# Gate of the delta branch applied in its PSUM bank, with the first operands of the output product taken from there, and a third up-projection job started early

## The chip, the cores and the metric

The kernel runs on one core of a Trainium2 chip, in one launch. The metric is the device time of one execution in microseconds (us), from the start of the program to its end. A profile of one execution gives the span from the first to the last instruction, the time of every instruction on its engine, and what each engine waited for. The engines are PE (TensorE, matrix products), PEld (its weight loads, which overlap the products), DVE (VectorE), ACT (ScalarE), POOL (GpSimd) and SP (SyncE, which issues nearly all of the DMAs).

## What is computed

One layer of a hybrid encoder on 512 tokens of 1024 channels, in float32:

```
h      = rmsnorm(x);  proj = h @ w_in          # pool | q k v z | gates
y_pool = pooled branch(p) @ pool_out
y_dn   = gated delta rule, both directions, normed @ dn_out
merged = sigmoid(g_pool) * y_pool + sigmoid(g_dn) * y_dn
x      = x + merged @ w_o
h2     = rmsnorm(x)
u      = conv3(h2 @ ffn_up);  x = x + (silu(gate) * value) @ ffn_down
out    = rmsnorm(x)
```

Everything around the change lies between `y_dn` and the first columns of `h2 @ ffn_up`.

## The kernel before

**Three products for one.** Every float32 operand is split into a rounded high part and a low part, the difference. `mm3` (lines 389 to 391) multiplies high by high, high by low and low by high into one PSUM bank. High parts are casts on ACT, low parts are subtractions on POOL or DVE. POOL cannot read PSUM.

**A planner writes the order.** Each step is declared with `A` (ACT), `V` (DVE), `G` (POOL), `M` (PE) or `L` (a DMA issued by SP), with an estimated cost, the names it reads and writes, and a key. The planner plays the program through with these costs; on each engine the ready step with the lowest key goes next. `FEED`, `EVICT` and `CHAIN` are offsets that put a step far ahead of plain keys; FEED goes before EVICT. The engines then run that order, each strictly in sequence, and wait on semaphores that the tile framework sets where instructions touch the same tile. Buffers come from rings: `pp` is a ring of three one-bank PSUM tiles, `raw`, `whi` and `wlo` hold weights (3, 2 and 2), `y` holds five 128x512 tiles, and `ms` two operand sets of the w_o product.

**The stage of `do_unit` (line 1530).** For each of eight channel blocks c, a job of 24 matmuls (8 contraction blocks, `mm3` each) forms a 128x512 block of y_dn in a `pp` bank, `ps_do`. Two loads bring the gate `gd` and the finished product of the pool branch `m1` into `y` tiles; ACT takes the sigmoid of `gd`. Then DVE multiplies the bank by the gate into the `gd` tile in SBUF (line 1546), which frees the bank, and adds `m1` into block c of the merged tile `m` (line 1549).

**The w_o product.** `merged @ w_o` runs as a scheme of seven half-size products, in the order 1, 2, 6, 5, 3, 7, 4 (`W_ORDER`). Each takes sums or differences of quarters of `merged` (tokens 0 to 255 and 256 to 511, channel blocks 0 to 3 and 4 to 7) and of `w_o`. The operands of products 1 and 2 are plain quarters; `s3` (for 7) is a first difference; those of 6, 5 and 3 are made in place in `m` by `mcombine` (line 1620). `msplit` casts an operand on ACT (line 1628) and takes its low part on DVE (line 1632). `wsum` (line 1588) forms the sums of w_o on DVE or POOL, `wsplit` (lines 1601 and 1604) their high and low parts; `LO_BY` says for each product and block which of POOL (G) and DVE (V) takes the low part. Their homes are tiles `ws` a and b and the freed tiles kT and kk.

**Where the products land.** A product has two token blocks j of four groups of `mm3`. Products 1, 6, 3 and 4 use the two banks of a single two-bank tile, `oo`, called `wo` in the trace; 2, 5 and 7 use `pp` banks (`ps_wo`). `wdone` says where each is added: `wplus` adds it to a half row of the residual tile `x2` (line 1753, `x` in the trace); `wkeep` copies product 1 to SBUF tile `wu` on ACT (line 1760); `wmore` adds 6 and 7 to `wu` on DVE (line 1765), and POOL adds `wu` to `x2` three times for each j.

**Into the next norm and the up projection.** `norm2_first` and `norm2_rest` (lines 1694 to 1716) form squares, root, reciprocal and scaled rows for 128 tokens at a time; PE turns them (line 1722), ACT and DVE split them into `h2` (lines 1728 and 1729). The up projection has 44 jobs of 24 matmuls; the first two (`up0_0`, `up0_1`) run in two halves of 256 tokens, since the first 256 tokens are normed before the rest. Each bank is taken by `conv3` (ACT line 1871, DVE line 1877) into a tile of pool `fp`, which `ffn_open` opens when the memory of the earlier stage is free (`tail` lists whose uses it awaits).

Of the kernel before, what the change touches and what calls it, by code (L numbers as in the profile page):

```python
# [14 lines left out]
P = 128  # L15
# [212 lines left out]
def hybrid_block(  # L228
# [55 lines left out]

    def G(cost, fn, r=(), w=(), key=0.0):
        add("pool", cost, fn, r, w, key)

# [135 lines left out]

    def job(src, kt, xs, xr, name, halves=False, pair=False, feed=None, more=0.0):

# [5 lines left out]
        if pair:  # L431
            def load():
                box["raw"] = wpool.tile([P, kt, n], F32, tag="wraw", bufs=RINGS["raw"], name=f"wr_{name}")
                sp.dma_start(box["raw"], src)

            def split():
                w = box["hi"] = wpool.tile([P, kt, 2 * n], F32R, tag="whi", bufs=RINGS["whi"], name=f"wp_{name}")
                act.copy(w[:, :, 0:n], box["raw"])

            def split2():  # L440
                w = box["hi"]
                pool.tensor_tensor(out=w[:, :, n:], in0=box["raw"], in1=f32(w[:, :, 0:n]), op=ALU.subtract)

            whi = f"whi:{name}"
            wlo = whi
            L(128, load, w=[f"raw:{name}"], key=FEED + u)
            A(ca(kt * n), split, r=[f"raw:{name}"], w=[whi], key=FEED + u)
            G(cp(kt * n), split2, r=[f"raw:{name}"], w=[whi], key=FEED + u)
        else:
            wb, whi, wlo = weights(src, kt, n, name, u, feed, more)  # L450
        pp = f"pp:{name}"

        def mmk(k, a, b):
# [3 lines left out]
            if pair:  # L457
# [7 lines left out]
                return  # L465
            mm3(box["ps"][:n, a:b], wb["hi"][:, k, :], wb["lo"][:, k, :], xhi[:, a:b], xlo[:, a:b], k == 0, k == kt - 1)

        spans = [(0, S)] if not halves else [(0, S // 2), (S // 2, S)]
        for i, (a, b) in enumerate(spans):
            for k in range(kt):  # L470
                lo_part = wlo if pair else f"{wlo}#{0 if k < kt // 2 else 1}"
                M((MM3 if not pair else 0.46) / len(spans), lambda k=k, a=a, b=b: mmk(k, a, b),
                  r=[whi, lo_part] + xr(k, a, b), w=[pp], key=u + 50 * i + k, n=4 if pair else 6)
        return box, pp, u
# [1056 lines left out]
    def do_unit(c):  # L1531
# [12 lines left out]

        def mul():
            dve.tensor_tensor(out=b["gd"], in0=box["ps"], in1=b["gd"], op=ALU.mult)

        def plus():
            dve.tensor_tensor(out=mg["m"][:, c, :], in0=b["gd"], in1=b["m1"], op=ALU.add)
# [16 lines left out]
    ADD = EVICT - 60  # L1566
    T_W = (slice(0, 256), slice(256, 512))
    u_wo = {p: next_unit() for p in W_ORDER}
    u_w0 = u_wo[1]
    wsets, wslot = {}, {}  # L1570

# [47 lines left out]
    def mcombine(dst, dstn, x, y, names, op, key, n):  # L1619
        V(cd(256 * n) + 0.22, lambda: dve.tensor_tensor(out=dst(), in0=x(), in1=y(), op=op), r=names, w=dstn, key=key)  # L1620

    def msplit(p, i, n, src, srcn, key):
# [36 lines left out]
    for i in range(0, QK, 2):  # L1659
        msplit(1, i, 2, *mblk(i, 0, 2), FEED + u_w0 + i)  # L1660
        mcombine(*s3(i), mblk(i, 0, 2)[0], mblk(i, 1, 2)[0], mblk(i, 0, 2)[1] + mblk(i, 1, 2)[1], ALU.subtract, FEED + u_w0 + i, 2)
    for i, n in ((0, 2), (2, 1), (3, 1)):
        msplit(2, i, n, *mblk(i + QK, 0, n), FEED + u_wo[2] + i)
    for i in range(0, QK, 2):
        (x, xn), (y, yn), (z, zn) = mblk(i, 0, 2), mblk(i, 1, 2), mblk(i + QK, 1, 2)
        mcombine(y, yn, y, z, yn + zn, ALU.add, FEED + u_wo[6] + i, 2)
        mcombine(x, xn, y, x, xn + yn, ALU.subtract, FEED + u_wo[6] + i, 2)
        msplit(6, i, 2, x, xn, FEED + u_wo[6] + i)
    for i in range(0, QK, 2):
# [77 lines left out]
    def wplus(p, j, th, n, u, eng=V):  # L1747
        t = 2 * th + j
        e, src, sn = (dve, lambda: wacc[p, j], wname(p, j)) if eng is V else (pool, lambda: wacc["u", j], f"y:wu{j}")

        def plus():
            dst = x2[t][:, half(n)]
            e.tensor_tensor(out=dst, in0=src(), in1=dst, op=ALU.add)

        eng(cd(512) if eng is V else cp(512), plus, r=[sn], w=[f"xr{t}#{n}"], key=u)

    def wkeep(j, u):
        def keep():
            wacc["u", j] = y_tile(f"wu{j}")
            act.copy(wacc["u", j], wacc[1, j])  # L1760
# [403 lines left out]
```

## Time and profile before

| what | value |
|---|---|
| median of three timed runs | 887.25 us (887.17 to 890.71) |
| the profiled execution | 886.23 us |
| its span, first to last instruction | 884.5 us |
| PE busy in the span | 867.1 us |
| granted TensorE clock, mean | 0.997 |

The profiled execution lies 1.02 us below the median, and 1.73 us of it lie outside the span. The views used below are the page of the profile, busy times by stretch (windows), the waits of PE, the instructions of a tile with their shortest, median and longest duration, and the timeline: start, duration, engine, line, tiles, and in brackets the idle time before, with what ended it.

### The profile page before, as it was taken

How to read it: one execution, taken by the hardware profiler on the slowest of the kernel's cores; microseconds unless marked ns; L12 is line 12 of the kernel's file. 1: busy time of each engine (PE TensorE's matmuls, PEld its weight loads, DVE VectorE, ACT ScalarE, POOL GpSimd, SP SyncE). 2: the span in 40 equal slices, each digit the busy share in tenths (PEclk: the TensorE clock that was granted, in tenths of full speed). 3: DMA queues.
4: the chain of work that ended last, by engine and by line, in shares of the span. 5: the costliest groups of instructions: out<-in, count | busy, mean ns of one | idle time of the engine just before them, and what ended most of it. 6: DMA issues, size and time to landing. Idle time of an engine off the chain costs nothing.

```text
span 884.5 us, 13820 instructions
## 1 busy us (share of the span) xinstructions
PE 867.1 (98%) x5027; PEld 729.3 (82%) x5027; DVE 602.2 (68%) x1025; ACT 471.1 (53%) x792; POOL 542.2 (61%) x463
## 2 busy tenths in 40 slices
PE   8999999999999999999999889999999999999997
PEld 7888888888888887888877669888888888888886
DVE  5756597367578887554768995565566555569996
ACT  6688544336858533346755555444443333465664
POOL 3445555223646554253699894787778776567763
PEclk9999999999999999999999999999999999999999
DMA  7365446304255463125896004566666675265553
GB/s 208 96 194 144 120 131 155 109 26 131 73 143 154 121 142 86 55 84 168 298 325 220 1 24 144 197 219 202 219 222 214 204 241 180 102 208 185 175 178 147
DMA packets 165511, 138.07 MB, mean 156 GB/s; under 512 B 23662, under 2 KB 133051, under 8 KB 165444
## 3 DMA queue, kind: packets, MB, share of 16 engines
q1 hardware_dynamic: 160706, 135.62, 49.4%
q10 hardware_dynamic: 4738, 1.58, 0.8%
q8 instruction: 39, 0.64, 0.3%
q14 instruction: 28, 0.23, 0.1%
HBM read 113.03 MB, written 24.15 MB: 155 GB/s over the span
## 4 chain that ended last, share of the span: by engine, by line
PE 62%; DVE 3%; ACT 1%; issue 0%; POOL 0%; DVEq 0%
PE ps_up L389 9%; PE ps_up L390 9%; PE ps_up L391 9%; PE dn L389 4%; PE dn L391 4%; PE dn L390 4%; PE ps_do L391 2%; PE ps_do L389 2%; PE ps_do L390 2%; PE ps_gp L389 1%; PE ps_gp L391 1%; PE ps_gp L390 1%; PE ps_p L389 1%; PE ps_po L391 1%; PE ps_po L389 1%; PE ps_po L390 1%
## 5 line engine op out<-in xcount | busy, mean ns | idle before, releaser
L415 POOL TENSOR_TENSOR wl_up<-wr_up,wh_up 128x512 fp32r<-128x512 f32 x88 | 117.0, 1350 | 46.4 <-ACT wh_up L411 46.3
L389 PE MATMUL ps_up<-h_hi,wh_up 128*128 128x512 f32 (+1 forms) x368 | 139.9, 380 | 0.0
L390 PE MATMUL ps_up<-h_lo,wh_up 128*128 128x512 f32 (+1 forms) x368 | 139.8, 380 | 0.0
L391 PE MATMUL ps_up<-h_hi,wl_up 128*128 128x512 f32 (+1 forms) x368 | 139.7, 380 | 0.0
L1877 DVE SCALAR_TENSOR_TENSOR c<-ps_up,fw,c 128x511 f32<-128x511 f32 x88 | 66.0, 750 | 98.1 <-ACT c L1871 92.0
L2066 POOL TENSOR_TENSOR w_dn<-wr_dn,w_dn 128x512 fp32r<-128x512 f32 x44 | 66.1, 1516 | 29.1 <-ACT w_dn L2063 25.9
L391 PEld LDWEIGHTS ps_up<-h_hi,wl_up 128*128 128x128 f32 x368 | 69.2, 188 | 13.2
L411 ACT CAST wh_up<-wr_up 128x1024 fp32r<-128x1024 f32 x44 | 46.3, 1051 | 63.5 <-PE ps_up L390 24.5
L389 PEld LDWEIGHTS ps_up<-h_hi,wh_up 128*128 128x128 f32 x368 | 69.2, 188 | 13.2
L390 PEld LDWEIGHTS ps_up<-h_lo,wh_up 128*128 128x128 f32 x368 | 69.2, 188 | 12.9
L1862 POOL TENSOR_TENSOR tp<-tp 128x512 f32<-128x512 f32 x44 | 60.8, 1382 | 15.6 <-DMA tp<-in_ffn_down_dram 11.6
L2063 ACT CAST w_dn<-wr_dn 128x512 fp32r<-128x512 f32 x69 | 42.4, 621 | 29.6 <-PE dn L391 19.1
L390 PE MATMUL dn<-w_dn,as 128*128 128x512 f32 x141 | 54.2, 385 | 0.0
L389 PE MATMUL dn<-w_dn,as 128*128 128x512 f32 x141 | 54.2, 384 | 0.0
L391 PE MATMUL dn<-w_dn,as 128*128 128x512 f32 x141 | 54.2, 384 | 0.0
L415 POOL TENSOR_TENSOR wl_k<-wr_k,wh_k 128x512 fp32r<-128x512 f32 x16 | 20.2, 1286 | 31.2 <-ACT wh_k L411 31.2
L1827 ACT CAST as<-a 128x512 fp32r<-128x512 f32 (+1 forms) x41 | 21.5, 534 | 32.0 <-DVE a L1898 28.4
L1831 DVE TENSOR_TENSOR as<-a,as 128x512 fp32r<-128x512 f32 (+1 forms) x41 | 38.5, 964 | 0.1
L415 POOL TENSOR_TENSOR wl_gp<-wr_gp,wh_gp 128x512 fp32r<-128x512 f32 x16 | 21.9, 1387 | 21.6 <-ACT wh_gp L411 21.6
L415 POOL TENSOR_TENSOR wl_v<-wr_v,wh_v 128x512 fp32r<-128x512 f32 x16 | 21.3, 1349 | 22.6 <-ACT wh_v L411 22.6
L1871 ACT ACTIVATE c<-ps_up,fw 128x512 f32<-128x512 f32 x44 | 33.9, 771 | 0.0
L1900 ACT ACTIVATE c<-c 128x512 f32<-128x512 f32 x22 | 13.9, 633 | 35.4 <-DVE c L1877 35.3
(394 smaller groups left out, 2528.6 us busy)
## 6 DMA issues: line engine op xcount, KB each, us to landing
wr_up<-in_ffn_up_dram SPq DMA_DIRECT2D x44, 512.0 KB, 3.9
tp<-in_ffn_down_dram SPq DMA_DIRECT2D x22, 512.0 KB, 4.7
t_scr<-tp SPq DMA_DIRECT2D x44, 256.0 KB, 2.7
wr_dn<-t_scr SPq DMA_DIRECT2D x20, 512.0 KB, 3.7
wr_dn<-in_ffn_down_dram SPq DMA_DIRECT2D x15, 512.0 KB, 3.6
x<-in_x_dram SPq DMA_DIRECT2D x8, 512.0 KB, 5.4
wr_k<-in_w_in_dram SPq DMA_DIRECT2D x8, 512.0 KB, 4.8
wr_z<-in_w_in_dram SPq DMA_DIRECT2D x8, 512.0 KB, 3.7
```

The costliest lines, as they stand in the source:

```text
L389: pe.matmul(ps, ahi, bhi, start=first, stop=False)
L390: pe.matmul(ps, ahi, blo, start=False, stop=False)
L391: pe.matmul(ps, alo, bhi, start=False, stop=last)
L411: act.copy(b["hi"], b["raw"])
L415: pool.tensor_tensor(out=b["lo"][:, sl], in0=b["raw"][:, sl], in1=f32(b["hi"][:, sl]), op=ALU.subtract)
L1827: act.copy(sets[p][:, i : i + n, 0, :], src())
L1831: dve.tensor_tensor(out=w[:, :, 1, :], in0=src(), in1=f32(w[:, :, 0, :]), op=ALU.subtract)
L1862: G(cp(512), lambda o=o, x=x, y=y: pool.tensor_tensor(out=w(*o), in0=w(*x), in1=w(*y), op=ALU.subtract), r=[n(*x), n(*y)], w=[n(*o)], key=u)
L1871: act.activation(b[j], box["ps"], AF.Identity, scale=fw[:, 1, ci : ci + 1], bias=fw[:, 3, ci : ci + 1])
L1877: dve.scalar_tensor_tensor(out=y[:, lo:hi], in0=box["ps"][:, lo + sh : hi + sh], scalar=fw[:, k, ci : ci + 1], in1=y[:, lo:hi], op0=ALU.mu ...
L2063: act.copy(b["w"][:, 0, :], raw["t"][:, j, :])
L2066: eng.tensor_tensor(out=b["w"][:, 1, :], in0=raw["t"][:, j, :], in1=f32(b["w"][:, 0, :]), op=ALU.subtract)
```

## The change

The bank of a `do_unit` is no longer left after the multiplication. Both DVE steps write back into it, and the operands of products 1 and 2 and the first sums are read from it:

```diff
-        def mul():
-            dve.tensor_tensor(out=b["gd"], in0=box["ps"], in1=b["gd"], op=ALU.mult)
-        def plus():
-            dve.tensor_tensor(out=mg["m"][:, c, :], in0=b["gd"], in1=b["m1"], op=ALU.add)
...
+        for n in ("gd", "m1"):
+            def into(n=n):
+                dve.tensor_tensor(out=box["ps"], in0=box["ps"], in1=b[n], op=ALU.mult if n == "gd" else ALU.add)
+            V(cd(512), into, r=[f"y:l{n}{c}"], w=[pp], key=FEED + u)
...
+        def keep():
+            act.copy(mg["m"][:, c, :], box["ps"])
+        def keep_hi():
...
+            act.copy(wsets[p][:, k, 0, :], box["ps"][:, 0:256])
+        def keep_lo():
+            w = wsets[p][:, k]
+            dve.tensor_tensor(out=w[:, 1, :], in0=box["ps"][:, 0:256], in1=f32(w[:, 0, :]), op=ALU.subtract)
+        A(ca(256), keep_hi, r=[pp, "pool:xp"], w=[ms], key=FEED + u)
+        A(ca(512), keep, r=[pp, "pool:xp"], w=[f"m{c}#0", f"m{c}#1"], key=FEED + u)
+        V(cd(256), keep_lo, r=[pp], w=[ms], key=FEED + u)
...
+        if p == 1:
+            V(cd(256), lambda: dve.tensor_tensor(out=mg["s3"][:, k, :], in0=box["ps"][:, 0:256], in1=mt(1), op=ALU.subtract),
+              r=[pp, nam(1)], w=[s3k], key=FEED + u)
+        else:
+            V(cd(256), lambda: dve.tensor_tensor(out=mt(0), in0=hi_ps(), in1=mg["s3"][:, k, :], op=ALU.subtract),
+              r=[pp, s3k], w=[nam(0)], key=FEED + u)
+            V(cd(256), lambda: dve.tensor_tensor(out=mt(1), in0=hi_ps(), in1=mt(1), op=ALU.add), r=[pp], w=[nam(1)], key=FEED + u)
```

For blocks 0 to 3 there is one such 128x256 sum, for blocks 4 to 7 two. The calls of `msplit` for products 1 and 2 and of `mcombine` for `s3`, 6 and 5 go; the one for product 3 stays. The estimated costs of `msplit` and `mcombine` rise to `cd(256 * n) + 0.5`.

The low parts of w_o change engine, and those on DVE get a key of the FEED class:

```diff
-    LO_BY = {1: (G, G, G, G), 2: (G, G, G, G), 6: (G, V, G, G), 5: (G, G, G, G), 3: (G, V, G, G), 7: (G, V, G, G), 4: (G, V, G, V)}
+    LO_BY = {1: (G, V, G, V), 2: (G, V, G, V), 6: (G, V, G, V), 5: (G, V, G, G), 3: (G, G, G, G), 7: (G, G, G, G), 4: (G, G, G, G)}
...
-    eng(cost, lo, r=[src[1], names[0]], w=[names[1]], key=key)
+    eng(cost, lo, r=[src[1], names[0]], w=[names[1]], key=key if eng is G else FEED + u_wo[p] - 40 + k)
```

The sums of w_o on POOL are held until block 0 of the `do` stage is finished (`after=["pp:do0"]`). Products 1 and 6 are joined in PSUM, and product 7 is added by DVE itself:

```diff
+    def wmore(j, u):
+        V(cd(512), lambda: dve.tensor_tensor(out=wacc[6, j], in0=wacc[6, j], in1=wacc["u", j], op=ALU.add),
+          r=[f"y:wu1{j}"], w=[wname(6, j)], key=u)
     def wdone(p, j, u):
-        if p == 1:
-            wkeep(j, u)
-        if p in (6, 7):
-            wmore(p, j, u)
-        for th, n in {1: ((0, 0),), 2: ((0, 0),), 6: (), 5: ((1, 1), (0, 1)), 3: ((0, 1),), 7: (), 4: ((1, 0),)}[p]:
+        if p == 6:
+            wmore(j, u)
+        if p in (1, 6):
+            wkeep(p, j, u)
+        for th, n in {1: ((0, 0),), 2: ((0, 0),), 6: ((0, 1),), 5: ((1, 1), (0, 1)), 3: ((0, 1),), 7: ((1, 1), (1, 0)), 4: ((1, 0),)}[p]:
             wplus(p, j, th, n, u)
-        for th, n in {6: ((0, 1),), 7: ((1, 1), (1, 0))}.get(p, ()):
-            wplus(p, j, th, n, u, G)
+        if p == 5:
+            for n in (1, 0):
+                wplus(p, j, 1, n, WORK + u_wo[4] + (40 if n else 50.5) + j / 10, G)
```

The copy of product 6 (with 1 in it) is what POOL adds to two half rows.

The job `up1_0` also runs in halves. Its weights are split into the tiles `ws` a, by `up_at`: one load, two casts of 128x512 on ACT and two low parts on POOL. The second half gets the lower key (`turn=-450`), so it comes ahead of the second halves of the first two jobs. The first three jobs are declared ahead of `tail`, so `ffn_open` awaits the uses of `ws` a by `up1_0` too:

```diff
+                  r=([whi] if pair else wn(k)) + xr(k, a, b), w=[pp], key=u + (50 + turn) * i + k, n=4 if pair else 6)
...
+    def up_job(c, j):
+        c0 = j * FFN + c * P
+        src, early_up = ffn_up[0][:, c0 : c0 + P], 2 * c + j < 3
+        kw = dict(halves=True, feed=WORK + u_wo[4] + 50 + 2 * c + j, at=up_at if c else None, turn=-450 if c else 0) if early_up else {}
+        return job(src, KD, hx2, hr2, f"up{c}_{j}", **kw)
+    first_jobs = {(c, j): up_job(c, j) for c, j in ((0, 0), (0, 1), (1, 0))}
```

More of the change, by code (lines that the diff above doesn't have):

```diff
@@ L283, in V, with G @@
         add("dve", cost, fn, r, w, key)
-    def G(cost, fn, r=(), w=(), key=0.0):
-        add("pool", cost, fn, r, w, key)
+    def G(cost, fn, r=(), w=(), key=0.0, after=()):
+        add("pool", cost, fn, r, w, key, after=after)
     def M(cost, fn, r=(), w=(), key=0.0, n=6):
@@ L422, in weights, with job @@
         return b, whi, wlo
-    def job(src, kt, xs, xr, name, halves=False, pair=False, feed=None, more=0.0):
+    def job(src, kt, xs, xr, name, halves=False, pair=False, feed=None, more=0.0, at=None, turn=0):
         n = src.shape[1]
@@ L449, in job @@
         else:
-            wb, whi, wlo = weights(src, kt, n, name, u, feed, more)
+            if at:
+                wk, wn = at(src, name, feed)
+            else:
+                wb, whi, wlo = weights(src, kt, n, name, u, feed, more)
+                wk = lambda k: (wb["hi"][:, k, :], wb["lo"][:, k, :])
+                wn = lambda k: [whi, f"{wlo}#{0 if k < kt // 2 else 1}"]
         pp = f"pp:{name}"
@@ L465, in mmk @@
                 return
-            mm3(box["ps"][:n, a:b], wb["hi"][:, k, :], wb["lo"][:, k, :], xhi[:, a:b], xlo[:, a:b], k == 0, k == kt - 1)
+            mm3(box["ps"][:n, a:b], *wk(k), xhi[:, a:b], xlo[:, a:b], k == 0, k == kt - 1)
         spans = [(0, S)] if not halves else [(0, S // 2), (S // 2, S)]
@@ L1513, in hybrid_block @@
     QK = KD // 2
+    T_W = (slice(0, 256), slice(256, 512))
+    wsets, wslot = {}, {}
     wr, mg = [None, None], {}
@@ L1566, in hybrid_block @@
     ADD = EVICT - 60
-    T_W = (slice(0, 256), slice(256, 512))
     u_wo = {p: next_unit() for p in W_ORDER}
     u_w0 = u_wo[1]
-    wsets, wslot = {}, {}
     def wo_load(n, kk):
@@ L1587, in wsum @@
         e, cost = (pool, cp(512) + 0.15) if eng is G else (dve, cd(512) + 0.3)
-        eng(cost, lambda: e.tensor_tensor(out=dst[0](), in0=x[0](), in1=y[0](), op=ALU.subtract),
+        more = {"after": ["pp:do0"]} if eng is G else {}
+        eng(cost, lambda: e.tensor_tensor(out=dst[0](), in0=x[0](), in1=y[0](), op=ALU.subtract), **more,
             r=[x[1], y[1], *(["pool:xp"] if dst[1][0] == "t" else [])], w=[dst[1]], key=key)
@@ L1619, in mcombine @@
     def mcombine(dst, dstn, x, y, names, op, key, n):
-        V(cd(256 * n) + 0.22, lambda: dve.tensor_tensor(out=dst(), in0=x(), in1=y(), op=op), r=names, w=dstn, key=key)
+        V(cd(256 * n) + 0.5, lambda: dve.tensor_tensor(out=dst(), in0=x(), in1=y(), op=op), r=names, w=dstn, key=key)
     def msplit(p, i, n, src, srcn, key):
@@ L1634, in msplit @@
         A(ca(256 * n), hi, r=srcn, w=names, key=key)
-        V(cd(256 * n) + 0.25, lo, r=srcn, w=names, key=key)
+        V(cd(256 * n) + 0.5, lo, r=srcn, w=names, key=key)
     s3 = lambda i: ((lambda: mg["s3"][:, i : i + 2, :]), [f"s3{i}", f"s3{i + 1}"])
@@ L1659, in hybrid_block @@
     for i in range(0, QK, 2):
[L1660 to L1668, printed above, removed]
+        msplit(6, i, 2, *mblk(i, 0, 2), FEED + u_wo[6] + i)
     for i in range(0, QK, 2):
@@ L1748, in wplus @@
         t = 2 * th + j
-        e, src, sn = (dve, lambda: wacc[p, j], wname(p, j)) if eng is V else (pool, lambda: wacc["u", j], f"y:wu{j}")
+        e, cost, src, sn = (dve, cd(512), lambda: wacc[p, j], wname(p, j))
+        if eng is G:
+            e, cost, src, sn = (pool, cp(512), lambda: wacc["u", j], f"y:wu6{j}")
         def plus():
@@ L1806, in ffn_open, with up_at, load, hi @@
         open_pool("fp")
+    def up_at(src, name, feed):
+        b = {}
+        wn = lambda k: [f"wsah{k // 4}", f"wsal{k // 4}"]
+        def load():
+            b["raw"] = wpool.tile([P, KD, P], F32, tag="wraw", bufs=RINGS["raw"], name=f"wr_{name}")
+            sp.dma_start(b["raw"], src)
+        def hi(i):
+            b[i] = [pools["mg"].tile([P, 4, P], F32R, tag=f"ws_{n}a{i}", name=f"w{n}_{name}{i}") for n in ("hi", "lo")]
+            act.copy(b[i][0], b["raw"][:, 4 * i : 4 * i + 4])
+        def lo(i):
+            pool.tensor_tensor(out=b[i][1], in0=b["raw"][:, 4 * i : 4 * i + 4], in1=f32(b[i][0]), op=ALU.subtract)
+        L(512, load, w=[f"raw:{name}"], key=feed)
+        for i in range(2):
+            A(ca(512), lambda i=i: hi(i), r=[f"raw:{name}"], w=wn(4 * i), key=feed)
+            G(cp(512), lambda i=i: lo(i), r=[f"raw:{name}", wn(4 * i)[0]], w=[wn(4 * i)[1]], key=feed)
+        return (lambda k: (b[k // 4][0][:, k % 4, :], b[k // 4][1][:, k % 4, :])), wn
+    def up_job(c, j):
[4 more added lines that the diff above has]
+    first_jobs = {(c, j): up_job(c, j) for c, j in ((0, 0), (0, 1), (1, 0))}
     tail = [b for b in plan.owner if b.split(":")[0] in ("y", "ms") or b[:2] in ("kT", "kk", "ws", "s3") or b[:3] == "t24"]
@@ L1888, in hybrid_block @@
         for j in range(2):
-            c0 = j * FFN + c * P
-            box, pp, u = job(ffn_up[0][:, c0 : c0 + P], KD, hx2, hr2, f"up{c}_{j}", halves=c == 0, feed=None if c else WORK + u_wo[4] + 50 + j)
+            box, pp, u = first_jobs.get((c, j)) or up_job(c, j)
             conv3(box, pp, j * NF + c, b, j, u)
```

23 lines of the change are left out of this document (11 added, 12 removed).

## The prediction

> **What bounds the kernel now.** I read the page first, then busy times by stretch, then the waits of PE, then the timeline at each wait.
>
> ```profile
> PE 867.1 (98%) x5027; PEld 729.3 (82%) x5027; DVE 602.2 (68%) x1025; ACT 471.1 (53%) x792; POOL 542.2 (61%) x463
> ```
>
> PE is busy nearly throughout, so only its idle time can be won. The columns of the windows are start and end, length, and busy time of PE, PEld, DVE, ACT and POOL, clock, DMA share:
>
> ```profile
> 436.00:481.50 45.50, 45.21 (x199) 36.88 (x198) 32.55 (x30) 25.35 (x39) 43.05 (x28) 1.00 0.96 313
> 481.50:531.00 49.50, 42.47 (x182) 32.04 (x181) 44.56 (x50) 26.53 (x54) 46.53 (x31) 1.00 0.04 11
> 531.00:544.30 13.30, 13.30 (x114) 13.28 (x113) 6.62 (x13) 6.21 (x13) 4.88 (x5) 1.00 0.26 81
> ```
>
> The `do` stage (436 to 481.5) and the first up jobs (531 to 544.3) leave PE nothing idle to speak of. The w_o stage between them leaves 7.0 us, with DVE (44.56 of 49.5) and POOL (46.53) both close to full. Who holds PE there (us in all, times, longest):
>
> ```profile
> PE wo L389 <- DVE x L1753: 3.0, 3, 1.5
> PE wo L391 <- DVE ms L1632: 1.8, 2, 1.3
> PE ps_wo L391 <- DVE ms L1632: 0.7, 1, 0.7
> PE wo L389 <- ACT wu L1760: 0.7, 1, 0.7
> PE wo L389 <- ACT ms L1628: 0.4, 1, 0.4
> PE ps_do L391 <- POOL wl_do L415: 0.3, 1, 0.3
> PE pt_b L1722 <- DVE sq L1712: 0.2, 1, 0.2
> PE pt_b L1722 <- ACT sq L1716: 0.2, 1, 0.2
> ```
>
> Eleven waits, 7.3 us idle. A wait costs more than its idle time:
>
> ```profile
> 484.03 0.39 PE L391 MATMUL wo<-ws_hi,ms 128*128 128x512 f32 x1
> 485.20 0.50 PE L389 MATMUL wo<-ws_hi,ms 128*128 128x512 f32 x1 [0.78 <-DVE x L1753]
> 485.53 0.39 PE L390 MATMUL wo<-ws_lo,ms 128*128 128x512 f32 x1
> ...
> 527.68 0.50 PE L389 MATMUL wo<-wq_kT,ms 128*128 128x512 f32 x1 [1.46 <-DVE x L1753]
> ```
>
> Matmuls start 0.23 us apart when nothing holds them; here 1.17 and then 0.33 pass, so 0.94 + 0.10 = 1.04 us go for 0.78 shown, 0.27 more per wait. Eleven waits cost 7.3 + 3.0 = 10.3 us. That is all that this change can remove.
>
> They are of two kinds. **Late operands**: the four waits on `ms` (2.9 us idle, 4.0 with restarts) are products 2 and 6 waiting for their operands. Here is why they are late, on DVE's timeline:
>
> ```profile
> 484.45 0.69 DVE L1753 TENSOR_TENSOR x<-wo,x 128x512 f32<-128x512 f32 x1 [0.46 <-PE wo L391]
> ...
> 485.39 0.68 DVE L1546 TENSOR_TENSOR gdl<-ps_do,gdl 128x512 f32<-128x512 f32 x1
> ...
> 490.85 1.78 DVE L1549 TENSOR_TENSOR m<-gdl,m1l 128x512 f32<-128x512 f32 x1
> ...
> 495.93 1.50 DVE L1632 TENSOR_TENSOR ms<-m,ms 128x256 fp32r<-128x256 f32 x1
> ```
>
> The last `do` job ends near 481.5; its block is multiplied at 485.4, merged at 490.9 and split by 497.4, 16 us for four short steps, since DVE is full of slow ones. **A shared tile**: the first row shows the other kind. The addition of block j=0 of product 1 waits until 484.45, for the matmul that began at 484.03; but that matmul belongs to the first group of j=1, in the other bank, and j=0 was complete. Then PE's next group waits for the addition, and the one after for ACT's copy of the same j=0. Reads of one bank of `wo` and matmuls into the other are made to alternate. Products 1 (two waits), 3 and 4 (one each) pay this.
>
> **The change part by part.** The durations (shortest, median, longest in ns):
>
> ```profile
> L1546 DVE TENSOR_TENSOR gdl<-ps_do,gdl x8: 679/688/692, 444.3 to 485.4; 128x512 f32<-128x512 f32 x8
> L1549 DVE TENSOR_TENSOR m<-gdl,m1l x8: 790/1692/1783, 445.0 to 490.8; 128x512 f32<-128x512 f32 x8
> L1632 DVE TENSOR_TENSOR ms<-m,ms x13: 415/1212/1778, 455.3 to 519.5; 128x512 fp32r<-128x512 f32 x11, 128x256 fp32r<-128x256 f32 x2
> L1620 DVE TENSOR_TENSOR m<-m x6: 678/1720/1780, 474.2 to 502.0; 128x512 f32<-128x512 f32 x6
> L1942 DVE TENSOR_TENSOR x<-dn,x x29: 403/677/692, 787.3 to 878.2; 128x512 f32<-128x512 f32 x27, 128x256 f32<-128x256 f32 x2
> L1628 ACT CAST ms<-m x13: 406/616/623, 454.6 to 516.3; 128x512 fp32r<-128x512 f32 x11, 128x256 fp32r<-128x256 f32 x2
> L1760 ACT COPY wu<-wo x2: 586/586/587, 486.2 to 489.3; 128x512 f32<-128x512 f32 x2
> ```
>
> DVE with one input in PSUM takes 0.68 us each time (half size 0.41); with both in SBUF 0.79 to 1.78.
>
> *Gate in the bank.* For each block, the multiplication stays at 0.68. The merge (median 1.69) becomes 0.68. What the bank now also carries: two ACT copies (0.41 and 0.59), one DVE low part (0.41) and one or two sums (0.41 each). No row of this trace has DVE writing to PSUM: I bound it by 0.68 and 1.78 and take 0.68, the row with the same inputs. From the end of the last job to its low part: 0.68 + 0.68 + 0.41 + 0.41, with handovers some 2.5 us, so about 484 in place of 497.4. Product 2 begins behind the seven groups left of product 1, at 481.5 + 7 x 0.68 = 486.3, or 488.4 with product 1's two waits. At 1.78 for both in-place steps the low part is there at 486.3, still in time. Product 6's own split must await the `ms` slot of product 1 (free near 488) and needs a cast (0.62) and a low part (1.21 to 1.78): near 491, with product 6 due near 493. All four waits go: **-4.0**. If two stay because DVE is still full, -2.0.
>
> The bank is held longer. The worst load of `m1` and the job that needs that bank back:
>
> ```profile
> 463.60 1.28 DVE L1549 TENSOR_TENSOR m<-gdl,m1l 128x512 f32<-128x512 f32 x1 [4.17 <-DMA m1l<-m_scr]
> ...
> 469.94 0.39 PE L389 MATMUL ps_do<-o_hi,wh_do 128*128 128x512 f32 x1
> ```
>
> From 463.60, 0.68 + 0.41 + 0.59 + 0.41 + 0.41 = 2.5 us end at 466.1, and job 6 takes the bank at 469.94: 3.8 us spare, cost nothing. Queued behind DVE's wait for that load are the first sums and low parts; nobody on PE awaits them for 20 us. ACT's casts of the next job's weights queue behind its new copies, about 1 us a block, with 25 of 45 us busy there.
>
> *DVE's load in the w_o stage.* The two merges left there (3.6 us) shrink to one of 0.68 with its sums, two of the four combines and two of twelve splits go, two low parts of weights go to POOL net, and four additions of 0.68 come: some 6 us less of 44.6. Product 4's second block waited 1.46 us because DVE came late to the first one's addition. That wait falls to the plain alternation of 0.78, and the two short ones on the turned rows mostly go: (1.46 - 0.78) + 0.4 + 2 x 0.27 = 1.6; I take **-1.4**, with 0 and -2.8 as ends.
>
> *Low parts between POOL and DVE.* POOL gives two each of products 1 and 2 to DVE, ahead of the stage, where DVE has 13 us free; the wait for `wl_do` (0.29 + 0.27) goes, **-0.5**, or stays.
>
> ```profile
> L1604 POOL TENSOR_TENSOR ws_lo<-wr_hi,ws_hi 128x512 fp32r<-128x512 f32 x11 | 17.9, 1645 | 3.6 <-ACT ws_hi L1601 3.6
> L1753 POOL TENSOR_TENSOR x<-wu,x x6: 1282/1484/1727, 505.1 to 528.7; 128x512 f32<-128x512 f32 x6
> ```
>
> Products 3, 7 and 4 bring POOL four more of 1.65, 6 and 5 two fewer, and `x` has two fewer of 1.48: its load in the stage stays near 46 us, while four low parts (6.6 us) less ahead let it begin earlier. So POOL can follow PE by some 6 us and no more: this caps the gain. The hold on `pp:do0` costs nothing: that bank was multiplied at 444.3 (first time in row L1546), and the first product that uses a sum made by POOL is 7, sixth in the order.
>
> *Products 6 and 7.* Product 7 lands in `pp` banks, two DVE additions of 0.68 in place of one and two POOL steps: no wait. Product 6 lands in `wo`. Before, its additions came after its last matmul; now DVE is early enough to begin on j=0 while j=1 runs (2.7 us). An addition into the bank, an addition to `x2` and ACT's copy are three steps, likely in two gaps of PE: two alternations at 1.04 as in product 1: **+2.0**. At 0 if DVE comes after j=1; +3.1 if each step has its own gap. Queued behind the in-place addition on DVE are the splits for 5 and 3, due 3 us later or more. The Trainium skill, "PSUM — Partial Sum Buffer", section "PSUM bank collisions raise a hardware error", says that accesses of two engines to one bank must be ordered, reads against reads included. No row here shows a DVE and an ACT read of one bank at once; by that rule the copy waits for the addition, 0.6 more, and the sum would be 0.6 us higher.
>
> *The third job in halves.*
>
> ```profile
> 531.02:533.89 2.87, 2.87 (x25) 1.00 0.01 3
> 544.29:549.76 5.47, 5.47 (x27) 1.00 0.62 207
> ```
>
> These are 24 half matmuls and 24 whole ones: two halves cost 2 x 2.87 - 5.47 = **+0.3**. Its first half adds 2.9 us of cover while tokens 256 to 511 are normed; PE had no idle time from 531 to 544.3, so it wins nothing by itself, but keeps that so when product 4 ends earlier. Its weights bring one load (the DMA share of the stage is 0.04), two casts and two POOL steps, needed last of all. `ffn_open` awaits its second half, which goes first of the three, so 5.7 us of the other two lie over the first `conv3`, one step of ACT and two of DVE:
>
> ```profile
> L1877 DVE SCALAR_TENSOR_TENSOR c<-ps_up,fw,c 128x511 f32<-128x511 f32 x88 | 66.0, 750 | 98.1 <-ACT c L1871 92.0
> ```
>
> ```profile
> L1871 ACT ACTIVATE c<-ps_up,fw 128x512 f32<-128x512 f32 x44 | 33.9, 771 | 0.0
> ```
>
> If that cover fails, PE waits these 2.3 us for a bank.
>
> **Sum:** -4.0 - 1.4 - 0.5 + 2.0 + 0.3 = **-3.6 us**. On the profiled execution, 886.23 - 3.6 = 882.6; the median of the runs is 1.02 higher, so I forecast **883.6**.
>
> **The rivals.**
> *No new alternation.* If DVE gets to product 6 only after its last matmul, and to products 1 and 3 later too, the +2.0 goes and about one more: -6.6, held by POOL's cap to -6, so **881.2**. For it: before, exactly this happened to product 6. Against: DVE loses 6 us of load, and takes the FEED splits no slower.
> *DVE and POOL still late.* The PE waits change names only, since POOL stays at 46 us of the stage. Then **887**. For it: POOL's row. Against: POOL holds PE in one wait of eleven.
> *The shared tile turns against it (slower).* Each read of `wo` j=0 that DVE does between PE's groups may have one two-SBUF step of 1.7 us ahead of it in DVE's queue. Product 6 has three such steps; at 1.04 + 1.7 each, 8.2 in place of 2.0 gives +2.6: **889.9**. It turns slower once the three cost more than 5.6 us together, that is once over 0.8 us stands ahead of each. Against: the steps follow each other on DVE, so one queue delay serves all.
> *The change doesn't do what it says* would be a stage in which `ms` waits stay: that is the second rival.
>
> **How the numbers follow.** Forecast 0.60 (its own range 881.2 to 886.0), no new alternation 0.17, still late 0.13, shared tile 0.10. The range takes in the first rival and the ends of the forecast and most of the second, and part of the last: 880.6 to 888.4. A measurement of this kernel can tell about 0.5%, 4.4 us, from no change. Below 882.8: a third of the forecast (0.20), nearly all of the first rival (0.15), and a little for terms sized too small: 0.38. Above 891.7: half of the last case at its worst: 0.05. The rest, 0.57, is within.
>
> **What would show it.** Right: no PE wait on `ms` for products 2 and 6; DVE rows `ps_do<-ps_do` at 0.68; PE waits in product 6 on DVE and ACT at `wo`; the last w_o matmul near 527.5 in place of 531.0; no idle PE in the halves. Wrong: in-place rows well above 0.7, PE waiting for a `pp` bank in the `do` stage, PE waiting on POOL for `wl_up` or low parts of 3, 7 or 4, or PE idle before the second job pair of the up projection.

## The result and the profile after

| | before | after |
|---|---|---|
| median of six runs each | 887.44 us (887.12 to 890.71) | 879.08 us (877.32 to 879.73) |
| ratio | | 0.9894, 95% interval 0.9875 to 0.9913 |
| the profiled execution, its span | 886.23 us, 884.5 us | 877.32 us, 875.5 us |
| first matmul of the `do` stage to the first of the up projection | 436.6 to 531.0: 94.4 us | 435.3 to 521.8: 86.5 us |
| from there to the end of the span | 353.5 us | 353.7 us |

The change is worth 8.4 us, more than twice the 3.6 of the forecast and beyond the low end of its range. In the two profiles it comes from the stretch around the change: 7.9 us there, and 0.2 us back afterwards. The remaining 1.3 us between the two profiles lies ahead of 435.3, where every engine executes the same instructions in the same order in both kernels, so it is no effect of the change.

The busy times by stretch of the kernel after (start and end, length, then PE, PEld, DVE, ACT, POOL, clock, DMA share, GB/s):

```profile
436.00:481.50 45.50, 45.50 (x202) 37.69 (x201) 31.71 (x48) 29.21 (x50) 39.49 (x28) 1.00 0.94 301
481.50:522.00 40.50, 38.36 (x175) 30.92 (x175) 35.58 (x47) 26.66 (x52) 38.30 (x28) 1.00 0.05 14
522.00:536.00 14.00, 14.00 (x122) 14.00 (x121) 6.62 (x10) 6.04 (x13) 5.93 (x5) 1.00 0.38 114
```

PE now idles 2.1 us in the w_o stage in place of 7.0, and nowhere else near it. The waits of PE from 436 to 560, the whole list:

```profile
PE wo L389 <- ACT wu L1783: 2.1, 2, 1.4
```

Eleven waits have become two. Their places, from the timeline of PE:

```profile
483.79 0.50 PE L389 MATMUL wo<-ws_hi,ms 128*128 128x512 f32 x1 [1.40 <-ACT wu L1783]
503.51 0.50 PE L389 MATMUL wo<-ws_hi,ms 128*128 128x512 f32 x1 [0.74 <-ACT wu L1783]
```

The first stands in product 1: j=1 waits for the addition and the copy of j=0. The second stands in product 3, whose j=0 waits for the copy of product 6. No wait on `ms` is left, none in product 6, none in product 4.

The steps on the bank, from the instructions of the tile `ps_do` (shortest, median, longest in ns, first and last start):

```profile
L1553 DVE TENSOR_TENSOR ps_do<-ps_do,gdl x8: 686/700/700, 443.0 to 479.1; 128x512 f32<-128x512 f32 x8
L1553 DVE TENSOR_TENSOR ps_do<-ps_do,m1l x8: 685/699/700, 443.8 to 483.0; 128x512 f32<-128x512 f32 x8
L1566 ACT CAST ms<-ps_do x8: 352/370/374, 444.8 to 485.3; 128x256 fp32r<-128x256 f32 x8
L1561 ACT COPY m<-ps_do x8: 582/591/594, 445.0 to 486.2; 128x512 f32<-128x512 f32 x8
L1570 DVE TENSOR_TENSOR ms<-ps_do,ms x8: 410/425/427, 445.7 to 486.8; 128x256 fp32r<-128x256 f32 x8
```

DVE writes back into the bank in 0.70 us, for 0.68 forecast. But the last block is less early than forecast. From DVE's timeline:

```profile
479.09 0.70 DVE L1553 TENSOR_TENSOR ps_do<-ps_do,gdl 128x512 f32<-128x512 f32 x1 [1.94 <-PE ps_do L391]
479.70 1.10 DVE L1633 TENSOR_TENSOR wq_kk<-t,wq_kT 128x512 fp32r<-128x512 f32 x1
480.72 1.77 DVE L1633 TENSOR_TENSOR wq_kk<-wr_lo,wq_kT 128x512 fp32r<-128x512 f32 x1
482.42 0.69 DVE L1776 TENSOR_TENSOR x<-wo,x 128x512 f32<-128x512 f32 x1
483.03 0.69 DVE L1553 TENSOR_TENSOR ps_do<-ps_do,m1l 128x512 f32<-128x512 f32 x1
483.76 0.42 DVE L1580 TENSOR_TENSOR m<-ps_do,s 128x256 f32<-128x256 f32 x1
485.72 0.42 DVE L1582 TENSOR_TENSOR m<-ps_do,m 128x256 f32<-128x256 f32 x1 [1.54 <-ACT ms L1566]
486.17 0.69 DVE L1776 TENSOR_TENSOR x<-wo,x 128x512 f32<-128x512 f32 x1
486.80 0.42 DVE L1570 TENSOR_TENSOR ms<-ps_do,ms 128x256 fp32r<-128x256 f32 x1
```

Two low parts of w_o and an addition stand between the multiplication and the merge, and then DVE waits 1.54 us for ACT's cast of this bank. The low part is there at 487.2, 8.1 us after the multiplication began, for 2.5 forecast. PE needs it in the fourth group of product 2, which begins near 488.0. The step that removes the `ms` waits arrives about a microsecond early, not four.

The surprise is product 6. Before and after, it runs in the two banks of `wo`. The rows around the end of it, PE and DVE together:

```profile
493.97 0.39 PE L391 MATMUL wo<-wq_kT,ms 128*128 128x512 f32 x1
494.20 0.40 PE L389 MATMUL wo<-wq_kT,ms 128*128 128x512 f32 x1
...
496.77 0.39 PE L391 MATMUL wo<-wq_kT,ms 128*128 128x512 f32 x1
...
497.20 0.70 DVE L1788 TENSOR_TENSOR wo<-wo,wu 128x512 f32<-128x512 f32 x1 [1.00 <-PE wo L391]
```

Block j=0 is complete with the matmul of 493.97. DVE is free 1.00 us before 497.20, just before the last of the four groups of j=1 begins at 496.30, so it comes in time for one gap, where the forecast had two. Yet it doesn't begin: it waits for the last matmul of j=1. Its addition stands behind j=1 in the written order, so DVE waits and PE doesn't.

### The profile page after: what moved, and what is told of

It is laid out like the page before. It is cut to its first block, busy times and chain, and to the rows that moved or that the text cites. A ratio compares the mean times of both kernels' runs of the same rounds, so it can differ in the third digit from the quotient of the medians.

```text
span 875.5 us, 13895 instructions
## 1 busy us (share of the span) xinstructions
PE 863.7 (99%) x5051; PEld 730.5 (83%) x5051; DVE 592.0 (68%) x1040; ACT 476.1 (54%) x806; POOL 530.1 (61%) x459
## 4 chain that ended last, share of the span: by engine, by line
PE 97%; DVE 2%; ACT 0%; issue 0%; DVEq 0%
PE ps_up L389 9%; PE ps_up L391 9%; PE ps_up L390 9%; PE dn L391 4%; PE dn L389 4%; PE dn L390 4%; PE ps_k L389 2%; PE ps_gd L389 2%; PE ps_k L391 2%; PE ps_k L390 2%; PE pw L1167 2%; PE ps_q L391 2%; PE ps_q L389 2%; PE ps_v L390 2%; PE ps_gd L391 2%; PE ps_z L391 2%
## 5 line engine op out<-in xcount | busy, mean ns | idle before, releaser
L415 POOL TENSOR_TENSOR wl_up<-wr_up,wh_up 128x512 fp32r<-128x512 f32 x86 | 112.0, 1323 | 53.2 <-ACT wh_up L411 53.2
L389 PE MATMUL ps_up<-h_hi,wh_up 128*128 128x512 f32 (+1 forms) x360 | 136.8, 380 | 0.0
L390 PE MATMUL ps_up<-h_lo,wh_up 128*128 128x512 f32 (+1 forms) x360 | 136.6, 380 | 0.0
L391 PE MATMUL ps_up<-h_hi,wl_up 128*128 128x512 f32 (+1 forms) x360 | 136.6, 380 | 0.0
L1884 DVE TENSOR_TENSOR as<-a,as 128x512 fp32r<-128x512 f32 (+1 forms) x41 | 40.6, 1015 | 0.1
```

Of the source, the lines that this page charges most:

```text
L389: pe.matmul(ps, ahi, bhi, start=first, stop=False)
L390: pe.matmul(ps, ahi, blo, start=False, stop=False)
L391: pe.matmul(ps, alo, bhi, start=False, stop=last)
L415: pool.tensor_tensor(out=b["lo"][:, sl], in0=b["raw"][:, sl], in1=f32(b["hi"][:, sl]), op=ALU.subtract)
L1884: dve.tensor_tensor(out=w[:, :, 1, :], in0=src(), in1=f32(w[:, :, 0, :]), op=ALU.subtract)
```

## The experiments

Times are medians, each beside the time of the kernel before that was taken together with it. Two theories divide them. **Order**: whether reads of `wo` alternate with matmuls into the other bank is settled by where the planner's costs and keys put them, and this change moved them behind j=1. **Load**: the waits went because DVE and POOL had less to do, and the order is a side matter.

**The shared tile alone, in the kernel before.** `wo` as two tiles of one bank each, nothing else:

```diff
-            wacc["oo"] = banks2("wo")
+            close_pool("oop")
+            open_pool("wop", space=bass.MemoryType.PSUM)
+            wacc["oo"] = [pools["wop"].tile([P, 512], F32, tag=f"wo{i}", name=f"wo{i}") for i in range(2)]
...
-wacc["oo"][:, j, :]
+wacc["oo"][j]
```

> The kernel before, with the two-bank tile wo replaced by two tiles of one bank each; the instruction order on every engine stays the same. Theory (the waits in products 1, 3 and 4 come from sharing one tile): PE's waits on DVE x and ACT wu go (3.0 and 0.7 us idle before), while the waits on ms stay and grow, because PE reaches them sooner and DVE is no earlier; 884 to 886.5 us against 887.4. Rival (DVE's queue is late for these steps anyway): the waits on x stay near 3 us and the time stays within 1 us of 887.4.

Measured: 885.71 us against 888.16, ratio 0.9976 (0.9964 to 0.9988). Its longest waits of PE from 436 to 560:

```profile
PE wo L394 <- DVE ms L1635: 2.8, 2, 2.0
PE pt_b L1725 <- DVE h_lo L1732: 1.3, 1, 1.3
PE ps_wo L394 <- DVE ms L1635: 0.7, 1, 0.7
PE wo L392 <- ACT ms L1631: 0.5, 1, 0.5
```

Every wait on `x` and `wu` is gone (3.7 us idle before). So the shared tile is what made them, as the prediction read it. But the waits on `ms` grew from 2.9 to 4.0 us: PE reaches the late operands sooner and waits there. Alone, this cure is worth 2.5 us.

**The same split in the kernel after.**

> The changed kernel with the same two one-bank tiles in place of wo, same order on every engine. Theory: its only two waits of this stage (on ACT wu, 1.40 in product 1 and 0.74 in product 3, 2.7 us with restarts) go, 876.4 us against 879.1. Rival (the copies or DVE are what is late): the two waits stay or come back elsewhere, 879 us.

Measured: 876.69 us against 888.16, ratio 0.987 (0.9848 to 0.9892). The whole list of waits from 436 to 560:

```profile
PE ps_up L394 <- POOL wl_up L418: 0.3, 1, 0.3
```

The two waits that the change left, 2.1 us and 0.5 of restarts, are gone, and the stretch falls from 86.5 to 84.0 us. This is the fastest version, better than both kernels by its profile; its interval and that of the change overlap, so the step between these two isn't shown by the times alone. The one wait left is on POOL, for 0.3 us, no longer than POOL held PE in the kernel before; the time is 11.5 us below it.

**The gate alone**: the kernel before with `do_unit`, the first operands and the first sums of the kernel after.

```diff
-            dve.tensor_tensor(out=b["gd"], in0=box["ps"], in1=b["gd"], op=ALU.mult)
-            dve.tensor_tensor(out=mg["m"][:, c, :], in0=b["gd"], in1=b["m1"], op=ALU.add)
+                dve.tensor_tensor(out=box["ps"], in0=box["ps"], in1=b[n], op=ALU.mult if n == "gd" else ALU.add)
...
+        A(ca(256), keep_hi, r=[pp, "pool:xp"], w=[ms], key=FEED + u)
+        A(ca(512), keep, r=[pp, "pool:xp"], w=[f"m{c}#0", f"m{c}#1"], key=FEED + u)
+        V(cd(256), keep_lo, r=[pp], w=[ms], key=FEED + u)
...
```

> The kernel before with the gate applied in the bank and the operands of products 1 and 2 and the first sums taken from it; low parts of w_o, joining of products 6 and 7, estimated costs and up jobs as before. Theory (late operands were the main loss, and DVE's load the reason of product 4's wait): no PE wait on ms in products 2 and 6, 881 to 883.5 us. Rival (the other edits carry the gain by giving DVE and POOL room): waits on ms stay in part, 885 us or more.

Measured: 884.28 us against 888.16, ratio 0.9951 (0.9933 to 0.997). Its first waits of PE:

```profile
PE wo L389 <- DVE x L1769: 2.4, 3, 0.9
PE pt_b L1738 <- DVE nst L1725: 1.4, 1, 1.4
PE wo L389 <- DVE wu L1781: 0.8, 1, 0.8
PE wo L389 <- ACT wu L1776: 0.7, 1, 0.7
PE wo L391 <- DVE ms L1566: 0.2, 1, 0.2
```

The waits on `ms` fall from 2.9 us to 0.4, not quite to the nothing that was expected. The gate does what the prediction said of it, and for about the price it gave: 3.9 us. All the alternations are still there, and product 6, which had none, now has one as well (`DVE wu`, 0.78 us at 499.77); the norm of the last tokens lies bare for 1.4 us.

**All but the gate**: the kernel after with the steps on SBUF of the kernel before, and its estimated costs.

```diff
-                dve.tensor_tensor(out=box["ps"], in0=box["ps"], in1=b[n], op=ALU.mult if n == "gd" else ALU.add)
+            dve.tensor_tensor(out=b["gd"], in0=box["ps"], in1=b["gd"], op=ALU.mult)
+            dve.tensor_tensor(out=mg["m"][:, c, :], in0=b["gd"], in1=b["m1"], op=ALU.add)
...
```

> The changed kernel with the gate, the operands of products 1 and 2 and the first sums made in SBUF as before (and the estimated costs of these splits as before); all other edits kept. Theory: the waits on ms come back, some 4 us, and DVE is full again, 883 to 886 us. Rival (the other edits carry the gain): 880 to 881 us.

Measured: 894.4 us against 888.16, ratio 1.0067 (1.0041 to 1.0092). Its two longest waits:

```profile
PE ps_wo L391 <- DVE ms L1637: 4.3, 2, 3.6
PE ps_up L389 <- DVE c L1914: 2.7, 1, 2.7
```

It is 8.4 us slower than the upper end expected. The gate alone gives -3.9 us and these other edits alone +6.2. Both kernels have the estimated costs of before, so their sum is to be set against the run with the old costs further down, which has both and gives -4.1. The parts don't add up: without the short steps on the bank the operands are late again (4.7 us of waits on `ms`), which would fit the low parts that go ahead on DVE with FEED keys, but no run takes these away alone. Beside the gate, all other edits together bring nothing that shows until the two costs are raised (-4.1 against -3.9). What the costs do without the other edits was not run.

**The order alone.** The kernel after, with the additions into `x2` and `wo` ahead of everything in the planner's order:

```diff
-    ADD = EVICT - 60
+    ADD = FEED - 1e5
```

> The changed kernel with one key changed: the additions and copies of the w_o products' banks go ahead of every other step on DVE and ACT, so that the reads of a block j=0 stand in the order between the matmuls of j=1. Nothing else is added. Theory (in the changed kernel products 6, 3 and 4 are free of alternation only because their reads stand behind the last matmul of j=1 in the order, while DVE works on splits): PE waits on DVE wo, DVE x and ACT wu appear in products 6, 3 and 4, +2 to +5 us, 881 to 884 us. Rival (DVE has become light enough, so such waits are gone wherever the reads stand): 878.5 to 879.5 us.

Measured: 887.87 us against 888.31, ratio 0.9999 (0.9988 to 1.001): the whole gain is gone, with the same instructions, and more than the 2 to 5 us expected. Its waits of PE from 436 to 560, all of them:

```profile
PE wo L389 <- ACT wu L1783: 2.8, 2, 1.4
PE ps_up L389 <- DVE c L1930: 2.7, 1, 2.7
PE wo L389 <- DVE x L1776: 2.2, 2, 1.4
PE wo L389 <- DVE wo L1788: 0.8, 1, 0.8
```

And product 6 on its timeline:

```profile
496.48 0.40 PE L391 MATMUL wo<-wq_kT,ms 128*128 128x512 f32 x1
496.91 0.70 DVE L1788 TENSOR_TENSOR wo<-wo,wu 128x512 f32<-128x512 f32 x1 [0.67 <-PE wo L391]
...
497.67 0.50 PE L389 MATMUL wo<-wq_kT,ms 128*128 128x512 f32 x1 [0.79 <-DVE wo L1788]
```

Here the forecast's alternation is seen: the addition to j=0 waits for a matmul into j=1, and the next matmul waits for the addition. Product 6 pays 0.79 (497.67) and 1.40 (500.73), with two restarts 2.7 us, for +2.0 forecast and 3.1 as its end. In all PE idles 5.8 us at `wo` in place of 2.1; with three more restarts of 0.27 that is 4.4 of the 4.7 us by which the stretch grew (91.2). The rest of the loss comes later: the third job's second half now goes last of the three, so the first `conv3` lies bare and PE waits 2.66 us for a bank, for 2.3 named as that price, and the clock falls behind that wait (last section).

**The same order with the split.**

> The same order of e5 with wo as two one-bank tiles. Theory: early reads cost nothing when the other bank is another tile, so the whole loss of e5 goes and the time is near that of e2, 876 to 878 us. Rival (the loss of e5, if any, is from splits coming later on DVE): the time stays at that of e5.

Measured: 883.83 us against 888.31, ratio 0.9954 (0.9939 to 0.9969). The longest waits:

```profile
PE ps_up L392 <- DVE c L1935: 2.7, 1, 2.7
PE pt_b L1746 <- DVE sq L1736: 1.7, 1, 1.7
PE ps_up L393 <- DVE h_lo L1753: 1.0, 1, 1.0
```

Every wait at `wo` is gone and the stretch is 85.7 us, below that of the change itself. The forecast of 876 to 878 us still fails: what stays of the loss is the bank wait and two in the norm. Split against split, the new keys cost 7.0 us (4.5 below the time before in place of 11.5), 1.7 of them in the stretch. So a bad order costs time without the shared tile too.

**The estimated costs alone.** The kernel after, with the planner's cost of `msplit` and `mcombine` as before. No instruction differs; only the order can:

```diff
-        V(cd(256 * n) + 0.5, lambda: dve.tensor_tensor(out=dst(), in0=x(), in1=y(), op=op), r=names, w=dstn, key=key)
+        V(cd(256 * n) + 0.22, lambda: dve.tensor_tensor(out=dst(), in0=x(), in1=y(), op=op), r=names, w=dstn, key=key)
...
-        V(cd(256 * n) + 0.5, lo, r=srcn, w=names, key=key)
+        V(cd(256 * n) + 0.25, lo, r=srcn, w=names, key=key)
```

> The changed kernel with the planner's estimates for msplit and mcombine as before (0.25 and 0.22 added in place of 0.5); no instruction is added or removed. Theory (order decides whether reads of wo alternate with matmuls): with DVE believed free sooner, some reads move between the matmuls of j=1, and PE waits on x, wo or wu return, 880 to 884 us. Rival (order of these steps doesn't matter while DVE is light): 878.5 to 879.5 us.

Measured: 883.29 us against 887.35, ratio 0.995 (0.9934 to 0.9967): half of the gain goes with two constants that no engine ever sees. The waits:

```profile
PE wo L389 <- ACT wu L1783: 2.8, 2, 1.4
PE wo L389 <- DVE x L1776: 1.2, 1, 1.2
PE wo L389 <- DVE wo L1788: 0.8, 1, 0.8
```

The timeline of PE at the end of product 6 and into the next shows one thing more:

```profile
498.55 0.50 PE L389 MATMUL wo<-wq_kT,ms 128*128 128x512 f32 x1 [0.79 <-DVE wo L1788]
...
500.91 0.80 PE L389 MATMUL wo<-wq_kT,ms 128*128 128x512 f32 x1 [1.40 <-ACT wu L1783]
501.51 0.63 PE L390 MATMUL wo<-wq_kk,ms 128*128 128x512 f32 x1
...
504.42 0.39 PE L391 MATMUL ps_wo<-wq_kT,ms 128*128 128x512 f32 x1
```

After the second wait the matmuls take 0.63 in place of 0.39 us for some 3.4 us: the clock is down. The account of the stretch, 91.2 us against 86.5: 4.8 us of idle time in place of 2.1 (+2.6), two more restarts (+0.5), 3.4 us at half the clock (+1.7), together +4.8 for +4.7 measured.

DVE's own row shows that it comes no later here than in the change:

```profile
497.79 0.70 DVE L1788 TENSOR_TENSOR wo<-wo,wu 128x512 f32<-128x512 f32 x1 [0.21 <-PE wo L391]
```

It is free for the addition 60.3 us after the first matmul of the `do` stage, and 60.9 us in the change. Only the place of the addition differs: here it waits for the second of the four groups of j=1, there for the last.

**The same costs with the split**, to see whether the lower costs hurt in any other way:

> The order of e9_old_costs (the planner's two costs at +0.25 and +0.22), with wo as two tiles of one bank. Theory (what e9 lost was only that reads of one bank of wo alternated with matmuls into the other): no PE wait on x, wu or wo at the wo matmuls, the stretch from the first ps_do matmul to the first ps_up matmul falls from 91.2 us to 85 or less, time 876 to 879. Rival (the lower costs put steps of DVE in a worse order, and the waits at wo were only where it showed): the waits move to ms or to the norm, the stretch stays at 88 or more, time 881 to 883.

Measured: 878.38 us against 887.14, ratio 0.9905 (0.9883 to 0.9926). The two longest waits, and none is at `wo` or `ms`:

```profile
PE pt_b L1746 <- DVE h_lo L1753: 0.6, 1, 0.6
PE pt_b L1746 <- ACT sq L1740: 0.2, 1, 0.2
```

What the costs had lost comes back with the tile split: 4.1 us below the time before become 8.8. The stretch falls from 91.2 to 85.9 us, a little above the 85 expected. So most of what the costs lost went through the alternation, but not all: split against split the stretch is 1.9 us longer with the old costs (85.9 against 84.0), of which the two waits above and their restarts are 1.3. In the times it is 8.8 against 11.5 us below the time before, with intervals that overlap.

**Smaller parts of the change**, each undone by itself in the kernel after:

The third job whole again:

```diff
-        src, early_up = ffn_up[0][:, c0 : c0 + P], 2 * c + j < 3
+        src, early_up = ffn_up[0][:, c0 : c0 + P], 2 * c + j < 2
...
-    first_jobs = {(c, j): up_job(c, j) for c, j in ((0, 0), (0, 1), (1, 0))}
+    first_jobs = {(c, j): up_job(c, j) for c, j in ((0, 0), (0, 1))}
```

> The changed kernel without the third up job in halves (up1_0 as in the kernel before). Theory (its first half covers the norm of the last 256 tokens, which e3 shows uncovered with a wait of 1.39 us): a PE wait of 1 to 2 us at the turned rows or the second halves, less 0.3 for the halves: 879.7 to 880.8 us. Rival (no cover needed, as in the kernel before): 878.5 to 879 us.

The joining of products 1, 6 and 7 as before (`wplus`, `wkeep`, `wmore`, `wdone`):

```diff
-        if p == 6:
-            wmore(j, u)
-        if p in (1, 6):
-            wkeep(p, j, u)
+        if p == 1:
+            wkeep(j, u)
+        if p in (6, 7):
+            wmore(p, j, u)
...
```

> The changed kernel with the joining of products 1, 6 and 7 as before (wu summed in SBUF by DVE, three additions on POOL for each block, none of product 7 on DVE directly). Theory: the last addition before the norm of tokens 256 to 511 goes through DVE and then POOL (0.7 and 1.5 us) again, and POOL gets two more steps: +1 to +2.5 us, 880 to 881.5 us, by waits at the turned rows or on POOL wl_up. Rival (that joining is off the path): 879 us.

The low parts of products 1 and 2 all on POOL:

```diff
-    LO_BY = {1: (G, V, G, V), 2: (G, V, G, V), 6: (G, V, G, V), 5: (G, V, G, G), 3: (G, G, G, G), 7: (G, G, G, G), 4: (G, G, G, G)}
+    LO_BY = {1: (G, G, G, G), 2: (G, G, G, G), 6: (G, V, G, V), 5: (G, V, G, G), 3: (G, G, G, G), 7: (G, G, G, G), 4: (G, G, G, G)}
```

> The changed kernel with all low parts of w_o for products 1 and 2 on POOL again (four more there, four fewer on DVE, ahead of the w_o stage). Theory (they give POOL room in the do stage and let its sums begin earlier): the wait on wl_do returns, 0.3 to 0.6 us, and POOL is some 6 us later in the stage, 879.5 to 881.5 us. Rival (POOL has room to spare): 879 us.

The gate in the bank, but the whole block copied to SBUF by ACT and the first operands and sums made there, with the estimated costs of before:

```diff
-        A(ca(256), keep_hi, r=[pp, "pool:xp"], w=[ms], key=FEED + u)
-        V(cd(256), keep_lo, r=[pp], w=[ms], key=FEED + u)
...
+    for i in range(0, QK, 2):
+        msplit(1, i, 2, *mblk(i, 0, 2), FEED + u_w0 + i)
...
```

> The changed kernel with the gate applied in the bank, but the bank then only copied to SBUF by ACT; the operands of products 1 and 2 and the first sums made from SBUF on DVE as before (estimated costs of these as before). All else as changed. Theory (the two-SBUF steps of 1.2 to 1.8 us make the operands late, not the multiplication's place): part of the waits on ms returns, 881 to 885 us. Rival (the merge in the bank alone is enough): 878.5 to 880 us.

| undone | us | before | below before | ratio and interval | waits of PE |
|---|---|---|---|---|---|
| nothing (the change) | 879.08 | 887.44 | 8.4 | 0.9894 (0.9875 to 0.9913) | `wu` 2.1 |
| third job | 880.76 | 888.31 | 7.6 | 0.9921 (0.9906 to 0.9936) | `wu` 2.1, then 0.7 and 0.3 in the up projection |
| joining | 881.38 | 888.31 | 6.9 | 0.9928 (0.9911 to 0.9945) | `wu` 1.4, POOL `wq_kk` 1.2, `x` 0.8, then 0.3 in the up projection |
| low parts of 1 and 2 | 881.65 | 887.35 | 5.7 | 0.9937 (0.9916 to 0.9958) | `wu` 1.4, `x` 1.2, `ms` 0.2 |
| operands from the bank | 883.42 | 887.35 | 3.9 | 0.996 (0.9944 to 0.9976) | `x` 2.2, `wu` 2.1, `ms` 0.6, turned rows 0.2 |

The intervals of the third job and of the joining overlap that of the change, so neither part is shown to be worth anything by itself. The third job's halves are seen in the waits, though: without them PE waits 1.0 us at the start of the up projection. With the joining of before, the new wait was for a low part of product 4 on POOL (`wq_kk`), not at the turned rows or for `wl_up` as expected. With the low parts on POOL the wait for `wl_do` didn't come back; other waits at `wo` came. The last row has the old costs as well: against the run with old costs alone (0.995, 0.9934 to 0.9967) it can't be told apart, so the copy by itself isn't shown to cost anything.

## Why the prediction failed

| step | forecast | measured in the profile |
|---|---|---|
| four waits on `ms` | -4.0 | -4.0: 2.9 idle and four restarts gone |
| product 4 and the turned rows | -1.4 (0 to -2.8) | -2.6: 1.46 + 0.37 idle, three restarts |
| `wl_do` | -0.5 | -0.6 |
| product 6 | +2.0 (0 to +3.1) | 0 |
| third job in halves | +0.3 | +0.2, all that lies behind the stretch |
| product 1, two waits into one | none | -0.3 |
| sum | -3.6 | -7.3; 7.7 by the two stretches, 0.4 not traced to a wait |

**The step that failed** is the one on product 6: "now DVE is early enough to begin on j=0 while j=1 runs", so "two alternations at 1.04 as in product 1". DVE was early enough for one gap, by 1.00 us, and no alternation came. A read of `wo` stands between PE's groups only if the planner puts it there, and the planner knows nothing of when DVE is free on the chip; it goes by its costs and keys. The change raises two costs by a quarter of a microsecond, and the prediction gave that edit no term. The runs show that it is worth 4.3 us (8.4 against 4.1), and that a change of keys alone is worth 8.0. With the costs of before, product 6 does alternate: 0.78 us by the gate alone, 0.79 and 1.40 with all other edits. The shared tile is what turns such an order into waits at `wo`: split it, and all of them go. It is not the whole price of an order, since among the split kernels 2.7 us (not clear of noise) and 7.0 us stay. The same step failed in product 4, where a "plain alternation of 0.78" was left and none remained. The size was right where an alternation does occur: 0.78 in product 4 and 2.7 us in product 6 of the run with the additions first.

**The rival "no new alternation"** had the result within 2.1 us, for a reason that didn't hold: DVE wasn't late. It was also cut off at 6 us by a cap that fell too. "Its load in the stage stays near 46 us" was wrong: POOL is busy 38.30 us of the stage after, against 46.53. It still fills its stage (38.30 of 40.50) but with 28 steps at 1.37 us of busy time each, where 31 took 1.50; why they are shorter was not isolated. A busy share near 95% was read as a fixed load. The version with the split runs 10.4 us shorter in the stretch than before, and POOL holds PE for 0.3 us behind it.

**What held.** Late operands: by the gate alone, waits on `ms` from 2.9 to 0.4 us and 3.9 us of time. The restart of 0.27 us per wait closes the accounts of two other runs to within 0.3 us. The price of a bare `conv3`, 2.3 us, was 2.66 where the third job's second half came last. On the timing of the last block the prediction was lucky: 8.1 us in place of 2.5, since two low parts with FEED keys and an addition stand ahead of the merge on DVE, and ACT's cast comes 1.54 us late; a microsecond or so more and product 2 would have waited. One reading was off without harm: 0.79 to 1.78 us for DVE steps with both inputs in SBUF leaves out the shortest in its own row L1620, 0.678.

**One bank, two readers.** The prediction weighed what the Trainium skill says in "PSUM — Partial Sum Buffer", section "PSUM bank collisions raise a hardware error": accesses of two engines to one bank must be ordered. The rows agree in product 1: DVE's addition runs from 482.42 to 483.11, and ACT's copy of the same bank begins at 483.15; the wait of PE behind both is 1.40 us, where a single step holds it 0.78. By that page product 6 would have paid 0.6 us more; in the run with the additions first it paid 0.7 more than the +2.0.

## What to carry to other kernels

Where two independent banks share one tile, a wait of the matrix engine on a reader of the *other* bank is a matter of the written order; split the tile, or put the readers behind the last matmul, before any work is taken off the engines. Where a planner writes the order, its estimated costs are part of the change: compare the places of the steps across engines first, and only then the durations. And a busy share close to one is no bound: look at whether that engine ever holds the critical one, and at the duration of its steps.

## What the runs showed of the hardware

**The clock fell after short waits.** In the run with the old costs the windows show a granted clock of 0.50 from 501 to 504, after idle times of 0.79 and 1.40 us that lie 1 us of work apart; in the kernel before with the split tile, the same after 0.46 and 1.98 us, and in the run with the additions first after a single wait of 2.66 us. The run with the same additions and the split tile has that same wait of 2.66 us, and its clock stayed at 1.00. In the run of all but the gate the clock fell after 3.58 us and again after 0.79 and 1.40 us, but not after 2.66 us. One window of the run with the old costs:

```profile
502.00:503.00 1.00, 1.00 (x4) 0.81 (x3) 0.33 (x1) 0.34 (x1) 0.40 (x1) 0.50 0.00 0
```

The Trainium skill, "TensorE: Matmul & The Clock Gate", section "What's actually happening", has the clock drop to a half after a whole idle window of about 3.4 us and come back after a busy one, and the window run freely. Half the clock agrees with these rows, and so does the 3.4 us that it lasted; that it takes a whole idle window doesn't, since all of these idle times but one are shorter. Waits of 2 to 2.7 us thus cost some 1.7 us more in some of these profiles (3.4 us at half the clock), and nothing more in others.

**DVE writes back into PSUM at almost no extra time**: 0.700 us (median of eight) for 128x512 in place in the bank, where the same operation with its result in SBUF took 0.688. ACT's cast of 128x256 took 0.370 us from the bank (median of eight) and 0.406 from SBUF (two in the kernel before).
